# Four squares in flight, a pause before each group of heads, and wider block sums in a hybrid encoder layer

## The chip, the cores and the metric

The kernel runs on one core of one Trainium2 chip. The metric is the time of one execution on the device in microseconds (us). The kernel before takes 2103.46 us, the median of three runs (2101.09 to 2105.57).

## The reference

One encoder layer is applied to two inputs with the same weights: the sample, 1024 tokens, and the prompt, 512 tokens, both of width 2048. Cut to what matters:

```python
def mixer_layer(x, ...):
    h = rms_norm(x, norm_g)
    z = h @ w_in                                  # 2048 -> 5632
    c_val, c_glu, c_gate, q, k, v, a_gate = split(z)
    q, k = apply_rope(q), apply_rope(k)           # 8 heads, 2 key/value heads, head size 128
    conv_out = conformer_conv(c_val, c_glu, ...) * silu(c_gate)   # 31 taps, layer norm, silu, @ w_pw
    attn_out = banded_sink_attention(q, k, v, sink) * silu(a_gate)  # blocks of 128, window 128
    mix = concatenate([conv_out, attn_out]) @ w_out               # 2048 -> 2048
    return x + mix

def encoder(x, ...):
    return rms_norm(mixer_layer(x, ...), final_norm_g)
```

All tensors are float32.

## The kernel before

Every product is made of three matmuls with rounded parts of the operands (high x high, high x low, low x high). The parts are made by `parts`: ScalarE (ACT) copies the high part (L486), VectorE (DVE) subtracts it (L487). The large products of the sample are done by blocks: a `Unit` takes two blocks of 128 output columns, half of the inner dimension and both halves of the tokens, and needs seven products (`STEPS`) instead of eight, of sums of blocks. A product is 4 x 3 = 12 matmuls (L197), a unit 84. After a product `tap` reads PSUM: ACT copies it (L223) or DVE adds it (L243; in `Onto`, the units of the output product, L290). Loads, stores and weights go through SP's queue in the order of the program that a scheduler sets; adding transfers go through POOL.

The order of work is written by hand in `encoder`. First come four stages of units for the sample's input product, `stages[0]` to `stages[3]` (eight units of the convolution's columns, first with one half of the inner dimension and then with the other; then the same for gates, keys, values and queries). Then come the prompt's 44 jobs `pj` (L631), the pointwise products of the convolution in two halves, the output product of the sample in two stages `over[0]` and `over[1]` of eight `Onto` units, and at last the prompt's own end (L1764).

Beside the matmuls run three lanes, `conv`, `attn` and `prep`. A lane holds generators. After every third matmul, `tick(3 * MM)` adds 648 (MM = 216, in ns) times the lane's `rate` to its credit; while the credit is positive, the first generator is stepped and what it yields is taken off. So a `yield 3000` at rate 1.3 is a pause of 3000 / 1.3 ns of this clock. `drain` steps a lane until it is empty, without a pause.

What the change touches:

- `rms_ahead` loads the rows of x by halves of a row block ([128, 1024], 512 KB) into tiles of the pool `F` (seven tiles, shared with everything else that is wide) and squares each on ACT with an accumulated sum (L859; the loads are L852). For the sample it runs on the lane `prep`, behind `sums_ahead`, from the fourth unit of `stages[0]` on at rate 1.3, and the lane is drained ahead of the last unit of that stage. The rate is 1.0 from the next stage on. For the prompt it runs in `stages[2]`.
- `spread_rms` turns the sample's result into a row over all partitions, R (L698 on DVE, L703 on PE, L874 on ACT), in three parts, which are called after the first three steps of the last unit of `stages[0]`. In the same unit `switch` loads and splits the tokens of the next stage, one sum of blocks after each step.
- `group` is the attention of one key/value head and its four query heads: it loads k and v (L1084) and the first block's q (L1096), pauses, splits k and v, and then does the blocks of 128 queries in `attention` (scores L1115, their maximum L1118, exponentials L1129, transposes L1149, products with v L1144). Two groups of the sample run on the lane `attn` from the first prompt job on (rate 1.8), `attention_sums` behind them, and then two groups of the prompt (rate 1.2). The lane is drained ahead of the last unit of `over[0]`.
- `conv_sums` reads the sample's gated convolution from DRAM by pairs of row blocks (L1262), makes the four block sums in place (`sums_in_place`, L1270 to L1273) and stores them for `over[1]`. It runs on the lane `prep` from the second step of the first unit of `over[0]` on, at rate 1.0.

Of the kernel before, what the change touches and what calls it, by code (L numbers as in the profile page):

```python
# [706 lines left out]
class Sequence:  # L707
# [136 lines left out]
    def rms_ahead(self):  # L844
        e, nc = self.e, self.e.nc
        held = deque()

        def load(n):
            if n < 2 * self.B:
                b, h = divmod(n, 2)  # L850
                held.append(e.F([D // 2]))
                nc.sync.dma_start(held[-1], self.xN[b * P : (b + 1) * P, h * D // 2 : (h + 1) * D // 2])  # L852

        load(0)
        load(1)
        yield LOAD
        for n in range(2 * self.B):
            x = held.popleft()
            nc.scalar.activation(x, x, AF.Square, accum_out=self.sq[:, n % 2, n // 2 : n // 2 + 1])  # L859
            load(n + 2)  # L860
            yield 3000
        v = e.small(self.B)
        nc.vector.tensor_tensor(v, self.sq[:, 0], self.sq[:, 1], ALU.add)
        nc.vector.tensor_scalar(v, v, 1.0 / D, RMS_EPS, ALU.mult, ALU.add)
        self.rcol = e.stat[self.s][:, 0 : self.B]
        e.rsqrt(self.rcol, v, self.B)
        yield 15000
# [205 lines left out]
    def group(self, g):  # L1073

        e, nc = self.e, self.e.nc
        if self.s == 0:
            k, v = ([e.T1([self.T]) for _ in range(2)] for _ in range(2))
        else:
            kv = e.F([2, self.T], F32R), e.F([2, self.T], F32R)
            k, v = [(t[:, 0], t[:, 1]) for t in kv]  # L1080
        held = []
        for src in (self.k_d[g], self.v_d[g]):
            held.append(e.A([self.T], F32))
            nc.sync.dma_start(held[-1], src)  # L1084
        self.load_query(g, 0)
        yield e.attn.rate * LEAD
        for dst in (k, v):
            e.parts(dst[0], dst[1], held.pop(0))
            yield 3500
        for b in range(self.B):  # L1090
            yield from self.attention(g, b, k, v)

# [117 lines left out]
class Mix:  # L1210
# [46 lines left out]
    def conv_sums(self):  # L1257
        e, nc = self.e, self.e.nc
        for j in range(HALF):
            x = [e.F([TS]) for _ in range(2)]  # L1260
            for t, k in zip(x, (j, j + HALF)):
                nc.sync.dma_start(t, self.xT[k])  # L1262
            yield 2 * LOAD
            self.sums_in_place(0, j, *x)
            yield 4000

    def sums_in_place(self, g, j, x0, x1):
        e, nc = self.e, self.e.nc
# [517 lines left out]
def encoder(ctx, tc, a):  # L1786
    e = Encoder(ctx, tc, a)
# [10 lines left out]
    stages = [  # L1798
        [plain] + [u(0, False) for u in conv[1:]],
        [u(1, True) for u in conv],  # L1800
        [u(1, False) for u in rest],
        [u(0, True) for u in rest],
    ]
# [83 lines left out]
    stages[0][-1].before.insert(0, e.prep.drain)  # L1887
    rms = sample.spread_rms()
    for step in range(SPREAD):
        stages[0][-1].after.setdefault(step, []).append(lambda: e.urgently(next, rms, None))  # L1890

    pace(stages[1][0], RATES[0])
    pace(stages[2][0], RATES[1])
# [55 lines left out]
    def prepare():  # L1949
        until(lambda: sample.convolved == NC, e.conv)  # L1950
        for half in halves:
            e.prep.add(half.prepare())
        e.prep.add(halves[0].fetch())
        e.attn.add(mix.attention_sums())
        for group in prompt.groups:
            e.attn.add(group)
# [113 lines left out]
```

## Time and profile before

| | |
|---|---|
| median of three runs | 2103.46 us (2101.09 to 2105.57) |
| the profiled execution | 2107.31 us, its span 2105.5 us |
| PE (matmul) busy | 2063.2 us, 98% of the span, 9234 matmuls |
| PE weight loads | 1689.4 us, 80% |
| DVE busy | 1751.4 us, 83% |
| ACT busy | 1043.0 us, 50% |
| POOL busy | 77.1 us, 4% |
| DMA | 494.54 MB, 235 GB/s in the mean |

PE is TensorE's matmuls, PEld its weight loads, SPq the queue of SyncE that issues transfers. A line of the timeline has the start in us, the duration in us, the engine, the source line, the instruction, what it writes and reads (names of tiles without numbers), the count, and in brackets the idle time of the engine just before it and what ended it. A line of groups ends in the busy time in us, the mean duration in ns, and the idle time before. Every source line is that of the kernel before.

### The profile page before, as it was taken

Reading aid. Unit: us, or ns where it says so; the run is one execution under the profiler, and the core shown is the slowest. Engines: PE = TensorE matmul, PEld = TensorE weight load, DVE = VectorE, ACT = ScalarE, POOL = GpSimd, SP = SyncE. Lnnn points to the kernel's source line nnn. Section 1 sums busy time; section 2 is a strip of 40 time slices with the busy share of each in tenths; the row PEclk is TensorE's granted clock in tenths of the full one; section 3 lists DMA queues with packets and bytes.
Section 4 is the critical chain, followed back from the end, with each engine's and each line's share of the span. In section 5 each row is a group of like instructions: output and inputs, shape, how many; then the busy total and the mean of one; then the engine's idle time right before and its main releaser. Section 6 shows DMA issues by size and latency. Waiting matters only on the chain. (4 is left out here: it accounts for less than half of the span.)

```text
span 2105.5 us, 26965 instructions
## 1 busy us (share of the span) xinstructions
PE 2063.2 (98%) x9234; PEld 1689.4 (80%) x9234; DVE 1751.4 (83%) x2855; ACT 1043.0 (50%) x1682; POOL 77.1 (4%) x92
## 2 busy tenths in 40 slices
PE   8999999999999999999999999999999999999996
PEld 6878888888887888788888888878888788788875
DVE  8758798998899999999476777677798988899866
ACT  6476435333454444554455777336554343455444
POOL 0001110000011111100000000000000000000000
PEclk9999999999999999999999999999999999999999
DMA  8988887865577767954455555996789898677898
GB/s 279 313 283 248 205 216 229 295 203 170 180 236 195 169 165 184 276 166 157 151 184 188 179 168 197 319 335 207 237 283 302 273 321 290 207 259 246 293 310 276
DMA packets 269914, 494.54 MB, mean 235 GB/s; under 512 B 23632, under 2 KB 107984, under 8 KB 269776
## 3 DMA queue, kind: packets, MB, share of 16 engines
q1 hardware_dynamic: 257104, 469.75, 67.5%
q0 software_dynamic: 12672, 23.07, 6.8%
q8 instruction: 72, 1.18, 0.2%
q14 instruction: 66, 0.54, 0.1%
HBM read 331.77 MB, written 160.96 MB: 234 GB/s over the span
## 5 line engine op out<-in xcount | busy, mean ns | idle before, releaser
L197 PE MATMUL a<-t,hl 128*128 128x512 f32 x2640 | 634.8, 391 | 8.1 <-ACT u L223 2.6
L197 PEld LDWEIGHTS a<-t,hl 128*128 128x128 f32 x2640 | 494.4, 188 | 116.6 <-ACT u L223 5.5
L486 ACT ACTIVATE hl<-raw 128x1024 fp32r<-128x1024 f32 (+1 forms) x356 | 323.9, 910 | 433.6 <-DVE raw L139 93.9
L487 DVE TENSOR_TENSOR hl<-raw,hl 128x1024 fp32r<-128x1024 f32 (+1 forms) x356 | 369.2, 1038 | 153.5 <-ACT hl L486 152.8
L631 PE MATMUL a<-t,hl 128*128 128x512 f32 x1344 | 328.1, 394 | 0.5 <-DVE hl L487 0.5
L197 PE MATMUL c<-t,hl 128*128 128x512 f32 x1320 | 320.2, 390 | 3.1 <-DVE u L290 2.6
L197 PEld LDWEIGHTS c<-t,hl 128*128 128x128 f32 x1320 | 247.0, 188 | 56.8 <-DVE u L290 4.3
L631 PEld LDWEIGHTS a<-t,hl 128*128 128x128 f32 x1344 | 248.2, 188 | 50.9 <-DVE hl L487 1.0
L999 DVE SCALAR_TENSOR_TENSOR f<-f,c_w_dw,f 128x512 f32<-128x512 f32 x248 | 175.2, 746 | 0.3
L631 PE MATMUL c<-t,hl 128*128 128x512 f32 x672 | 165.5, 394 | 0.0
L962 DVE SCALAR_TENSOR_TENSOR f<-f,c_w_dw,f 128x512 f32<-128x512 f32 x232 | 163.7, 745 | 1.2 <-ACT f L957 1.2
L631 PE MATMUL b<-t,hl 128*128 128x512 f32 x672 | 163.4, 392 | 0.2 <-DVE hl L487 0.2
L197 PE MATMUL b<-t,hl 128*128 128x512 f32 x660 | 160.0, 390 | 0.0
L631 PEld LDWEIGHTS b<-t,hl 128*128 128x128 f32 x672 | 125.0, 188 | 25.3 <-DVE hl L487 0.6
L631 PEld LDWEIGHTS c<-t,hl 128*128 128x128 f32 x672 | 125.1, 189 | 24.4
L197 PEld LDWEIGHTS b<-t,hl 128*128 128x128 f32 x660 | 123.7, 188 | 25.5
L991 DVE SCALAR_TENSOR_TENSOR f<-f,w_both,f 128x512 f32<-128x512 f32 x120 | 89.8, 748 | 1.8
L223 ACT ACTIVATE u<-a 128x512 f32<-128x512 f32 x82 | 48.6, 592 | 57.4 <-PE a L197 55.3
L394 ACT ACTIVATE hl<-raw 128x1024 fp32r<-128x1024 f32 x44 | 46.5, 1056 | 59.6 <-PE a L631 22.3
L223 ACT ACTIVATE g<-a 128x512 f32<-128x512 f32 x78 | 46.2, 593 | 56.1 <-PE a L197 54.1
L1129 ACT ACTIVATE p<-p,tiny 128x384 f32<-128x384 f32 (+1 forms) x96 | 54.6, 570 | 38.3 <-DVE tiny L1126 28.0
L486 ACT ACTIVATE a<-pt 128x512 fp32r<-128x512 f32 x64 | 37.9, 592 | 67.9 <-PE pt L1149 67.6
(332 smaller groups left out, 2561.4 us busy)
## 6 DMA issues: line engine op xcount, KB each, us to landing
raw<-w_in SPq DMA_DIRECT2D x171, 512.0 KB, 5.1
raw<-wsum_P SPq DMA_DIRECT2D x32, 512.0 KB, 4.7
raw<-w_out SPq DMA_DIRECT2D x31, 512.0 KB, 5.5
raw<-w_pw SPq DMA_DIRECT2D x24, 512.0 KB, 4.4
raw<-w_out SPq DMA_DIRECT2D x48, 256.0 KB, 5.3
wsum_P<-raw SPq DMA_DIRECT2D x47, 256.0 KB, 3.4
f<-x_s SPq DMA_DIRECT2D x16, 512.0 KB, 7.3
a<-sum_S SPq DMA_DIRECT2D x24, 256.0 KB, 5.6
```

Source lines behind the costliest of these rows:

```text
L197: nc.tensor.matmul(acc, hl[:, l, o, j, :], toks[j][:, r], start=name in FRESH and j == 0 and q == 0, stop=name in LAST and j == HALF - 1 a ...
L223: nc.scalar.activation(t, bank, AF.Copy)
L394: e.nc.scalar.activation(t[:, 0], raw, AF.Copy)
L486: nc.scalar.activation(hi, x, AF.Copy)
L487: nc.vector.tensor_tensor(lo, x, hi.bitcast(F32), ALU.subtract)
L631: nc.tensor.matmul(job.acc[0], hl[:, l, kk // HALF, kk % HALF, :], r, start=i == 0 and p == 0, stop=i == nk - 1 and p == 2,)
L962: nc.vector.scalar_tensor_tensor(t, h[:, j : j + T], w(j), t, ALU.mult, ALU.add)
L991: nc.vector.scalar_tensor_tensor(m0, odd[:, j : j + H], both(j), m0, ALU.mult, ALU.add)
L999: nc.vector.scalar_tensor_tensor(out, d[:, j : j + H], w(2 * j + k), out if j else m0, ALU.mult, ALU.add)
L1129: nc.scalar.activation(p[:, 0:n], p[:, 0:n], AF.Exp, bias=nm[:, h : h + 1], accum_out=l[:, h : h + 1])
```

## The change

Four edits:

- In `rms_ahead` the sample has four loads of x in flight instead of two; the prompt keeps two.
- In `group` a pause of `e.attn.rate * 4000` is put between the split of k and v and the first block, that is 4000 ns of the lanes' clock at any rate.
- In `conv_sums` the pause after each pair is 20000 instead of 4000.
- In `encoder` the three parts of `spread_rms` follow the second to the fourth step of the last unit of `stages[0]` instead of the first to the third.

```diff
@@ rms_ahead
-        load(0)
-        load(1)
+        ahead = 2 if self.s else 4
+        for n in range(ahead):
+            load(n)
         yield LOAD
         for n in range(2 * self.B):
             x = held.popleft()
             nc.scalar.activation(x, x, AF.Square, accum_out=self.sq[:, n % 2, n // 2 : n // 2 + 1])
-            load(n + 2)
+            load(n + ahead)
             yield 3000
@@ group
         for dst in (k, v):
             e.parts(dst[0], dst[1], held.pop(0))
             yield 3500
+        yield e.attn.rate * 4000
         for b in range(self.B):
             yield from self.attention(g, b, k, v)
@@ conv_sums
             yield 2 * LOAD
             self.sums_in_place(0, j, *x)
-            yield 4000
+            yield 20000
@@ encoder
     rms = sample.spread_rms()
     for step in range(SPREAD):
-        stages[0][-1].after.setdefault(step, []).append(lambda: e.urgently(next, rms, None))
+        stages[0][-1].after.setdefault(step + 1, []).append(lambda: e.urgently(next, rms, None))
```

## The prediction

> **What bounds the kernel now.** I read the head of the page first, then stretches of 20 us, then the matrix engine's waits, and then the timeline round each wait.
>
> ```profile
> span 2105.5 us, 26965 instructions
> PE 2063.2 (98%) x9234; PEld 1689.4 (80%) x9234; DVE 1751.4 (83%) x2855; ACT 1043.0 (50%) x1682; POOL 77.1 (4%) x92
> ...
> 120.00:140.00 20.00, 19.17 (x85) 15.50 (x84) 8.92 (x12) 14.58 (x27) 0.00 (x0) 1.00 0.90 302
> 140.00:160.00 20.00, 17.49 (x69) 13.45 (x68) 15.67 (x43) 15.11 (x27) 0.00 (x0) 0.91 0.72 247
> ...
> 180.00:200.00 20.00, 20.00 (x90) 16.57 (x89) 15.39 (x23) 11.88 (x18) 2.73 (x3) 1.00 0.85 250
> ```
>
> The columns of a stretch are PE, PEld, DVE, ACT and POOL busy, then the granted clock, the DMA share and GB/s. An undisturbed stretch holds 90 matmuls, 0.222 us each, and such stretches fill most of the span. So PE is the bound, and no matmul is taken away by the change. All that can be gained is PE's idle time, 2105.5 - 2063.2 = 42 us, and matmuls slowed by a lower clock. Of the 42 us those at the very start and the very end are not touched. What PE waits for is in the waits of PE; the first column after the colon is the total, the last the longest.
>
> ```profile
> PE c L197 <- DVE u L290: 2.6, 4, 1.2
> PE a L197 <- ACT g L223: 2.5, 1, 2.5
> PE s L1115 <- DVE tiny L1118: 2.5, 1, 2.5
> PE s L1115 <- ACT a L486: 2.2, 1, 2.2
> ```
>
> Three of these four are single waits, so the question is which edit reaches which.
>
> **Four squares ahead.** The first stage ends so:
>
> ```profile
> 124.43 5.76 PE L197 MATMUL a<-t,hl 128*128 128x512 f32 x24 [0.83 <-ACT u L223]
> ...
> 130.71 0.58 SPq L852 DMA_DIRECT2D f<-x_s  x1
> ...
> 136.25 0.33 SPq L120 DMA_DIRECT2D raw<-w_in  x1
> ...
> 136.62 0.91 SPq L852 DMA_DIRECT2D f<-x_s  x2
> ...
> 144.61 1.06 ACT L859 ACTIVATE f<-f 128x1024 f32<-128x1024 f32 x1 [3.65 <-DMA f<-x_s]
> 145.66 0.58 ACT L223 ACTIVATE g<-a 128x512 f32<-128x512 f32 x1
> ...
> 146.29 7.36 PE L197 MATMUL a<-t,hl 128*128 128x512 f32 x24 [2.51 <-ACT g L223]
> ```
>
> The last two loads of x leave at 136.62, after a weight load at 136.25 that stood ahead of them on SP. ACT comes to the fifteenth square, waits 3.65 us for its rows, and the copy of a product out of PSUM (L223) stands behind the square; PE needs that bank and stands 2.51 us. Then 24 matmuls take 7.36 us where the same 24 took 5.76 at 124.43: 1.60 us more, with the clock of the stretch down to 0.91. The wait of 0.83 at 124.43 is of the same kind. Sum: 0.83 + 2.51 + 1.60 = 4.9 us.
>
> [...]
>
> After the change the squares keep their places, but load n+4 is issued where load n+2 was, two squares (6000 of the lane's counter at rate 1.3, 4.6 us) earlier. The last pair then takes the place of the loads before it, of which 130.71 is the last: 5.9 us earlier than 136.62, ahead of the weight load, and 5.9 covers a wait of 3.65. The price is DMA time and SP's queue, past which these loads move:
>
> ```profile
> f<-x_s SPq DMA_DIRECT2D x15, 512.0 KB, 7.4
> raw<-w_in SPq DMA_DIRECT2D x4, 512.0 KB, 6.4
> ...
> 100.00:110.00 10.00, 10.00 (x46) 8.29 (x45) 7.81 (x11) 6.18 (x11) 0.00 (x0) 1.00 0.97 340
> ...
> 130.00:140.00 10.00, 10.00 (x46) 8.26 (x44) 1.69 (x3) 6.76 (x14) 0.00 (x0) 1.00 0.95 321
> 140.00:150.00 10.00, 7.49 (x26) 5.75 (x25) 6.34 (x10) 5.95 (x10) 0.00 (x0) 0.83 0.73 251
> ...
> 120.60 1.23 DVE L487 TENSOR_TENSOR hl<-raw,hl 128x1024 fp32r<-128x1024 f32 x1 [6.24 <-ACT hl L486]
> ```
>
> Two loads are 1.05 MB, at 340 GB/s 3.1 us of DMA time pulled out of 140 to 150, where the share is 0.73, into a stretch of 0.95 and more. Weights behind them land up to 3.1 us later. Cover: the split that ends at 121.83 is first used by the second half of the 24 matmuls, about 127.3, so 5.5 us. So this price is 0 as long as the cover holds, and I take 0, since PE lost no matmul from 100 to 110 at 0.97 (46 in 10 us); its far end is a rival below, and a gain beyond the waits is excluded, since PE cannot run ahead of its own 0.222 us. The prompt keeps its two loads.
>
> **Spreading the rms one step later.** The same instructions move back by one step of 12 matmuls, 2.7 us:
>
> ```profile
> L698 DVE TENSOR_SCALAR u<-c_ident,tinyr 128x128 fp32r<-128x128 f32 x8 | 1.8, 283 | 0.0
> ...
> L703 PE MATMUL s<-u,ones_r 128*128 128x512 f32 x4 | 1.8, 448 | 0.0
> ```
>
> L698 has two such groups, 3.6 us of DVE in all, and these now meet one more set of token splits. They issue no DMA. R is first read in the next stage, five steps on. The stretch in which they fall has DVE at 15.67 of 20, so the cost may be nothing, or less, since the step that they leave has just been waiting for the square root; the other end is the longest wait of PE for DVE's additions above, 1.2 us. I take 0.3 lost, nearer to the room that the stretch shows.
>
> **4000 more before each group of heads.** Both sequences wait at the start of their first group, and not of their second:
>
> ```profile
> 880.00:900.00 20.00, 17.50 (x81) 14.42 (x82) 19.73 (x37) 9.50 (x18) 0.00 (x0) 1.00 0.68 220
> ...
> 891.73 1.03 PE L1115 MATMUL s<-t,a 128*128 128x256 f32 x6 [2.48 <-DVE tiny L1118]
> ...
> 1414.89 1.25 SPq L1096 DMA_DIRECT2D u<-q_d  x2
> ...
> 1420.54 0.63 ACT L486 ACTIVATE a<-u 128x512 fp32r<-128x512 f32 x1 [1.89 <-DMA u<-q_d]
> ...
> 1421.22 0.74 PE L1115 MATMUL s<-f,a 128*128 128x256 f32 x4 [2.22 <-ACT a L486]
> ```
>
> The pause is 4000 ns of the clock that counts 216 ns a matmul, 18.5 matmuls or 4.1 us of PE. A pause issues nothing itself; the k, v and q loads stand ahead of it as before. At 1421 the cause is a transfer, q of 1414.89 landing at 1420.5; 4.1 us of other matmuls ahead cover 2.22 us, and I take all of it. At 891 the cause is DVE with 19.73 of 20 us busy: a full engine is as far behind 4 us later unless what fills it is the split of k and v. From 0 to 2.5; I take a quarter, 0.6.
>
> What the pauses move: two groups of the sample and two of the prompt are in one lane, so the last block comes 4 x 4.1 = 16.5 us later.
>
> ```profile
> 1681.06 0.53 SPq L480 DMA_DIRECT2D att_d<-u  x1
> ...
> 1706.11 5.60 PE L197 MATMUL a<-t,hl 128*128 128x512 f32 x24
> ...
> L1118 DVE CUSTOM_DVE_ANT_0 p<-s,c_mask,c_attn_sink 128x256 f32<-128x256 f32 (+1 forms) x32 | 16.4, 546 | 2.7 <-PE s L1115 2.6
> L487 DVE TENSOR_TENSOR a<-pt,a 128x512 fp32r<-128x512 f32 x20 | 13.7, 687 | 5.6 <-ACT a L486 5.6
> ...
> 1640.00:1660.00 20.00, 19.85 (x97) 16.59 (x98) 20.00 (x40) 5.56 (x9) 0.00 (x0) 1.00 0.81 262
> ```
>
> The last unit of the output's first half begins within the 24 matmuls of 1706.11, at 1708.9, and runs the lane dry; the last block would end at 1697.6, 11 us ahead. But 16.5 us more of attention lies in a stage where DVE is full (20.00). The two groups are of the stretch 1421 to 1682, which holds the prompt's eight blocks (32 reductions, four a block): 30.1 / 8 = 3.8 us of DVE a block, a block every 33 us. So 16.5 us is half a block, 1.9 us of DVE, or a whole one, 3.8, if a block's edge falls so. On a full engine that is 0 to 3.8 us of PE (less than nothing is excluded: no work leaves this stage by the pauses); I take 1.9 lost, the half block.
>
> **Block sums over their stage.** In that stage DVE waits for the sums' rows and holds up the additions that free PSUM:
>
> ```profile
> 1613.87 0.69 DVE L1270 TENSOR_TENSOR f<-f,f 128x512 f32<-128x512 f32 x1 [1.73 <-DMA f<-mix_d]
> ...
> 1632.33 0.32 SPq L1262 DMA_DIRECT2D f<-mix_d  x1
> ...
> 1635.14 0.69 DVE L1270 TENSOR_TENSOR f<-f,f 128x512 f32<-128x512 f32 x1 [2.35 <-DMA f<-mix_d]
> ...
> 1638.42 0.96 PE L197 MATMUL c<-t,hl 128*128 128x512 f32 x3 [1.25 <-DVE u L290]
> ...
> 1640.15 0.74 PE L1144 MATMUL pv<-a,f 128*128 128x512 f32 x2 [0.55 <-DVE a L487]
> ```
>
> Row pairs come one behind the other because the tiles of the pair before are still being stored. With 9000 + 20000 instead of 9000 + 4000 a pair, a pair's buffers are free long before the next is read. The two waits shown take 1.25 + 0.55 of PE, the one at 1613.87 another 0.2: 2.0 us, which I take whole; from 0 to 2.0. The four sums end at 9 + 3 x 29 = 96 us of lane clock, and the seven units to the drain hold about 122, so the drain finds nothing.
>
> **Sum.** -4.9 + 0.3 - 0.6 - 2.2 + 1.9 - 2.0 = -7.5 us. The profiled execution took 2107.31 us (span 2105.5 and 1.8 around it), so it would take 2099.8. That execution lies 3.85 above the median 2103.46; the median becomes 2096.0.
>
> **Rivals.** *The queue was the limit.* If squares wait because DMA is full (0.97 at 100 to 110), loads issued earlier only wait longer, and the 4.9 stay: 2103.46 - 2.6 = 2100.9. For it: the share. Against it: 136.62 came late for SP's order, not for DMA's.
>
> *Weights starve, slower.* The loads of x stand ahead of raw<-w_in, and a weight load that lands past its cover of 5.5 us stops PE. Three units lie in the stretch. A stop of 3.1 us with the 1.60 of slow matmuls is 4.7 us, at three units 14.1, and the 4.9 are not won: 2103.46 - 2.6 + 14.1 = 2115.0. It decides once weights need 6.4 + 5.5 = 12 us to land instead of 6.4. Against it: at 0.97 PE lost nothing from 100 to 110. [...]
>
> *The moved attention eats it.* The pauses move waits but remove none, the sums gain nothing on a full DVE, and the 3.8 us are paid: 2103.46 - 4.9 + 0.3 + 3.8 = 2102.7. For it: 20.00 of 20. Against it: most of that stage's stretches hold their matmuls.
>
> **How the numbers follow.** Forecast 0.60; queue the limit 0.15; attention eats it 0.11; weights starve 0.14. A measurement here tells about 0.2%, 4.2 us, from no change. The forecast lies below 2099.3, faster; I give faster 0.62 (a little of the second case), same 0.24, slower 0.14. Best end: all waits gone at no price, 4.9, 2.5, 2.2 and 2.0, makes 11.6, so 2091.9. The top takes in 2102.7 and the 2.1 us by which a run here lay above the median: 2104.8. The case at 2115 is left out.
>
> **What would show it.** In the changed profile: no wait of a square above 1 us for x_s, PE's wait of 2.51 gone and the clock 1.00 from 140 to 160, with 88 or more matmuls (step one); no L1115 wait near 1430 (step two); L1270 without waits for mix_d and the sums spread to about 1680 (step three); the last att_d store at about 1690 to 1698. Wrong would be: ACT waits for raw<-w_in before 150; a wait for DVE of over 2 us between 1560 and 1710; attention work crowded at the last unit; or single waits of 2 us at new places.

## The result, and the profile after

The changed kernel takes 2112.58 us, the median of 17 runs (2109.03 to 2118.79), against 2106.96 us for the kernel before in 17 runs beside it. The ratio is 1.0025 with a 95% interval of 1.0016 to 1.0034: slower by 5.3 us, where 7.5 us faster was forecast. The profiled execution took 2117.92 us, 5.3 us above its median, so it shows more loss (10.6 us of span) than the medians do.

The head of the page of the changed kernel, and two of its stretches of 20 us (PE, PEld, DVE, ACT and POOL busy, granted clock, DMA share, GB/s):

```profile
span 2116.1 us, 26976 instructions
PE 2067.0 (98%) x9234; PEld 1693.4 (80%) x9234; DVE 1752.1 (83%) x2855; ACT 1044.1 (49%) x1682; POOL 77.2 (4%) x92
...
140.00:160.00 20.00, 17.25 (x74) 13.38 (x73) 15.90 (x43) 16.32 (x29) 0.00 (x0) 1.00 0.76 257
...
1710.00:1730.00 20.00, 17.48 (x72) 14.07 (x71) 15.26 (x24) 12.78 (x21) 0.00 (x0) 0.91 0.91 309
```

The same instructions are there, and PE's idle time has grown from 42 to 49 us. From 140 to 160 it does 74 matmuls, not the 88 that were to show step one. New is the stretch 1710 to 1730 with 72, which in the kernel before held 90, with its transfers already at a share of 0.99:

```profile
1710.00:1730.00 20.00, 20.00 (x90) 16.57 (x89) 18.70 (x29) 16.82 (x28) 0.00 (x0) 1.00 0.99 331
```

The waits of PE in the changed kernel, by what ended them (total, times, longest):

```profile
PE a L197 <- ACT u L223: 3.5, 4, 1.6
PE s L1117 <- ACT a L486: 3.5, 1, 3.5
PE a L197 <- DVE u L290: 3.0, 3, 1.3
PE a L197 <- DVE g L290: 2.5, 1, 2.5
...
PE a L197 <- ACT g L223: 1.7, 2, 1.5
PE s L1117 <- DVE tiny L1120: 1.7, 2, 1.2
```

Line numbers after line 855 have grown by one and after 1089 by two: L1117 is the scores of L1115, L860 the square of L859. The wait for the scores that was to go from 2.22 to nothing is 3.5. The wait of 2.5 for `g` (L290) did not exist before.

The timeline of the changed kernel at the three places, first the squares:

```profile
125.37 5.74 PE L197 MATMUL a<-t,hl 128*128 128x512 f32 x24 [1.63 <-ACT u L223]
...
136.49 0.33 SPq L120 DMA_DIRECT2D raw<-w_in  x1
136.86 0.91 SPq L852 DMA_DIRECT2D f<-x_s  x2
...
144.56 1.06 ACT L860 ACTIVATE f<-f 128x1024 f32<-128x1024 f32 x1 [2.62 <-DMA f<-x_s]
...
146.25 2.11 PE L197 MATMUL a<-t,hl 128*128 128x512 f32 x8 [1.54 <-ACT g L223]
...
1415.64 0.93 SPq L1085 DMA_DIRECT2D a<-k_d  x1
...
1424.89 0.89 PE L1117 MATMUL s<-f,a 128*128 128x256 f32 x4 [3.51 <-ACT a L486]
```

The last pair of x leaves at 136.86, where it left at 136.62, and again behind the same weight load. Nothing has been loaded earlier. The load of k leaves at 1415.64 (before: 1410.97, with the kernel 2 us behind), and the scores still come too early for it.

Then the edge between the two halves of the output product, first the first token loads of the next half in the kernel before, and then the changed kernel:

```profile
1676.36 1.36 SPq L839 DMA_DIRECT2D p<-mix_d  x3
```

```profile
1697.12 0.86 SPq L839 DMA_DIRECT2D p<-mix_d  x2
...
1701.20 0.56 SPq L480 DMA_DIRECT2D att_d<-u  x1
...
1715.67 0.86 SPq L839 DMA_DIRECT2D a<-msum_S  x2
...
1716.57 0.43 SPq L271 DMA_DIRECT2D g<-xT_s  x1
...
1722.91 1.31 ACT L486 ACTIVATE t<-a 128x512 fp32r<-128x512 f32 x2 [2.39 <-DMA a<-msum_S]
...
1724.13 1.04 ACT L486 ACTIVATE hl<-raw 128x1024 fp32r<-128x1024 f32 x1
1725.37 0.69 DVE L290 TENSOR_TENSOR g<-a,g 128x512 f32<-128x512 f32 x1 [3.55 <-issue]
...
1726.20 3.19 PE L197 MATMUL a<-t,hl 128*128 128x512 f32 x7 [2.52 <-DVE g L290]
```

The last attention block is stored at 1701.20 instead of 1681.06. The loads of the next half's tokens (L839), which go into tiles that this block held, leave between 1697 and 1746 instead of 1676 and 1733. In that crowd (DMA share 0.97 from 1716 to 1726) the rows of `g`, issued at 1716.57, are used only at 1725.37, 8.8 us later (the trace has them landed at 1725.29; in the kernel before, rows of `g` issued at 1708.25 took 4.1 us); DVE is idle until then (3.55, for which the row names no releaser), ACT waits 2.39 for token rows with a weight split queued behind them (1724.13), and PE stands 2.52 us and its granted clock is 0.50 for 3.41 us from 1725.69 on.

### The profile page after: what moved, and what is told of

Same layout as the page of the kernel before. It is cut to its first block, busy times and chain, and to the rows that moved or that the text cites. A ratio compares the mean times of both kernels' runs of the same rounds, so it can differ in the third digit from the quotient of the medians.

```text
span 2116.1 us, 26976 instructions
## 1 busy us (share of the span) xinstructions
PE 2067.0 (98%) x9234; PEld 1693.4 (80%) x9234; DVE 1752.1 (83%) x2855; ACT 1044.1 (49%) x1682; POOL 77.2 (4%) x92
## 4 chain that ended last, share of the span: by engine, by line
PE 71%; DMA 10%; DVE 10%; issue 5%; ACT 2%; POOL 1%; SPq 1%; ACTq 0%; DVEq 0%; POOLq 0%
PE a L197 20%; PE a L631 12%; PE c L197 10%; PE c L631 6%; PE b L631 6%; PE b L197 5%; DVE hl L487 2%; PE pv L1146 2%; PE s L1117 2%; PE s L197 2%; PE a L1766 2%; DMA f<-x_s 1%; PE pt L1151 1%; DMA raw<-w_out 1%; DMA raw<-wsum_P 1%
## 5 line engine op out<-in xcount | busy, mean ns | idle before, releaser
L197 PE MATMUL a<-t,hl 128*128 128x512 f32 x2640 | 635.5, 391 | 13.2 <-ACT u L223 3.5
L197 PEld LDWEIGHTS a<-t,hl 128*128 128x128 f32 x2640 | 493.7, 188 | 123.2 <-ACT u L223 6.1
L197 PE MATMUL c<-t,hl 128*128 128x512 f32 x1320 | 321.1, 391 | 1.7 <-DVE u L290 1.3
L197 PEld LDWEIGHTS c<-t,hl 128*128 128x128 f32 x1320 | 248.1, 188 | 54.9 <-DVE u L290 2.5
L197 PE MATMUL b<-t,hl 128*128 128x512 f32 x660 | 160.5, 390 | 0.0
L197 PEld LDWEIGHTS b<-t,hl 128*128 128x128 f32 x660 | 123.7, 188 | 25.4
```

The lines of the kernel that those rows point to most:

```text
L197: nc.tensor.matmul(acc, hl[:, l, o, j, :], toks[j][:, r], start=name in FRESH and j == 0 and q == 0, stop=name in LAST and j == HALF - 1 a ...
```

## The experiments

Eighteen kernels were run, each in five rounds beside the kernel before. The table gives the ratio to before with its interval, and in us how much more (+) time than before the profiled execution took for the same matmuls of a stretch (matmuls weighted by their columns; the stretches are named by their times in before). A single stretch scatters: the fifteen other profiles whose order is that of before up to 165 took 0.5 to 3.3 us less than before for 118 to 165, 1.7 in the mean. So only differences of 3 us and more, or ones that come back in several kernels, are read.

| kernel | ratio (95%) | 118-165 | 1050-1130 | 1400-1450 | 1500-1552 | 1552-1665 | 1665-1765 |
|---|---|---|---|---|---|---|---|
| whole change | 1.0025 (1.0016-1.0034) | -0.5 | 1.1 | 3.0 | 1.9 | -2.9 | 6.5 |
| e1 loads and rms | 0.9996 (0.9984-1.0008) | -0.9 | 0.0 | 2.3 | 0.0 | -2.1 | 0.4 |
| e2 pause | 1.0060 (1.0043-1.0076) | -2.0 | 1.2 | 3.6 | 1.2 | 7.1 | 5.0 |
| e3 sums 20000 | 1.0011 (1.0002-1.0019) | -1.9 | -0.1 | 0.0 | 0.0 | -4.1 | 8.2 |
| e4 pause, prompt | 1.0024 (1.0014-1.0034) | -1.6 | 0.0 | -0.3 | -0.1 | 0.2 | 2.9 |
| e5 pause, sums' stores on POOL | 1.0037 (1.0023-1.0051) | -2.0 | 1.4 | 2.3 | 2.9 | 2.0 | 2.8 |
| e6 sums' stores on POOL | 1.0000 (0.9987-1.0014) | -1.1 | 0.0 | -0.1 | 0.0 | -0.9 | 0.9 |
| e7 pause, sample | 1.0021 (1.0007-1.0035) | -0.5 | 1.2 | 4.8 | -0.1 | -0.8 | 2.2 |
| e8 attention earlier | 1.0033 (1.0021-1.0044) | -2.2 | 0.2 | -1.1 | 2.9 | -1.8 | 0.9 |
| e9 sums 20000 on POOL | 1.0007 (0.9996-1.0018) | -1.1 | 0.0 | 2.5 | 0.0 | -3.7 | 3.0 |
| e10 sums 12000 | 1.0000 (0.9988-1.0011) | -1.8 | 0.0 | 3.2 | 0.0 | -3.8 | 1.5 |
| e11 sums 12000 on POOL | 1.0003 (0.9992-1.0014) | -3.3 | -0.1 | 1.7 | 0.0 | -3.5 | 3.7 |
| e13 x on POOL | 1.0003 (0.9991-1.0015) | -5.3 | 0.0 | 0.6 | 0.0 | 3.2 | 0.3 |
| e14 edge rows on POOL | 1.0010 (0.9999-1.0022) | -2.6 | -0.1 | -0.2 | 0.0 | 0.0 | 3.6 |
| e15 change, edge rows on POOL | 1.0036 (1.0020-1.0052) | -2.4 | 1.4 | 1.7 | 2.3 | -3.2 | 9.3 |
| e16 e13 and e14 | 1.0014 (1.0004-1.0025) | -5.3 | -0.1 | 1.6 | 0.0 | -1.0 | 5.6 |
| e17 last x on POOL | 1.0018 (1.0006-1.0029) | 2.8 | 0.0 | 2.1 | 0.2 | -1.8 | 0.7 |
| e18 e17 and e10 | 1.0014 (1.0003-1.0025) | 1.2 | -0.1 | 0.2 | 0.0 | -2.1 | 4.6 |

(e12 changes the order from 1390 on and is told below.)

### The parts alone

**e1**, four loads ahead and the rms one step later:

```diff
+        ahead = 2 if self.s else 4
...
+            load(n + ahead)
...
-        stages[0][-1].after.setdefault(step, []).append(...)
+        stages[0][-1].after.setdefault(step + 1, []).append(...)
```

> Four loads of x ahead and the rms one step later, without the pause and with the old block sums. The prediction's terms for these two were -4.9 and +0.3, together -4.6 us. The two traces speak against both: every engine has the same instructions in the same order in both kernels up to 876 us. Theory 'nothing moved' (mine): the same program in all but names, so the same time as before, within 2 us, and ACT waits again 2 us or more for the last rows of x. Rival 'the loads are worth their price': -3 to -5 us. Rival 'weights starve': +4 us or more, with ACT waiting for raw<-w_in.

Level with before, as the first theory said. The instructions of every engine come in the same order as before from end to end. Why shows in the trace of before, at the seventh to tenth loads:

```profile
113.91 1.06 ACT L859 ACTIVATE f<-f 128x1024 f32<-128x1024 f32 x1 [0.27 <-DMA f<-x_s]
114.77 2.66 SPq L852 DMA_DIRECT2D f<-x_s  x4
...
117.98 1.06 ACT L859 ACTIVATE f<-f 128x1024 f32<-128x1024 f32 x1 [1.91 <-DMA f<-x_s]
```

The square of 113.91 is the fifth; by 117.4 ten loads have left (two up to 101.38, four from 104.05 to 110.53, and these four). Five are in flight, with a program that asks for two. The scheduler already runs the loads further ahead than that; the text of the program does not set the depth.

**e2**, the pause alone, and **e4** and **e7**, before the prompt's groups and before the sample's alone:

```diff
+        yield e.attn.rate * 4000
...
+        if self.s:
+            yield e.attn.rate * 4000
...
+        if not self.s:
+            yield e.attn.rate * 4000
```

> The pause before each group of heads alone. The prediction's terms were -0.6 -2.2 +1.9 = -0.9 us. Theory 'late attention' (T1): the last block ends about 20 us later (1701 instead of 1681), the tiles that it holds are those into which the rows of the third stage are read, and PE waits for these rows at the stage's edge, 2 us or more near 1726 with a second of half clock; so all of the loss is here, +5 us or more. Rival 'late sums' (T2): the late rows are those of the block sums, so the pause alone costs 0 to 2 us, and the wait near 1726 is gone.

> The pause only before the prompt's two groups; the sample's two groups start as before. The last block then ends about 8 us later than before, not 16.5 to 20. T1: about half of the loss of the full pause, +2 to +4 us, and the wait near 1726 shorter than with the full pause. Rival 'the sample's groups' (T3), by which the loss of the full pause comes from the new waits between 892 and 1425 (1.2, 0.9, 0.7 and 3.5 us with half clock): nothing is lost here, 0 to -2 us, and the wait at 1425 is shorter than the 2.22 us before.

> The pause before the sample's two groups only, the complement of the pause before the prompt's (+0.24%). T3 (the loss is where the sample's groups start): new waits of about 1 us at 892 to 1076, 3.4 us at 1422, +3 us or more by 1450, and little after. T1 (only late attention near the end costs): nothing until 1500, and then the loss of half the shift, +2 to +5 us between 1600 and 1760. If the parts add up, pause (+12.6) less pause before the prompt (+4.1 to +5) leaves +7.5 to +8.5; if less comes out, the two shifts together make a collision that neither makes alone.

The pause alone costs 12.6 us, more than twice the whole change; the prompt's half 5.1, the sample's half 4.4. So each half costs something (both theories were half right), and the 3 us that are left, no more than the intervals allow for, would come only of both together. At the edge e4 and e7 lose 2.9 and 2.2, with the last block stored at 1691.0 and 1692.5; e2, with 1709.1, loses 5.0. The five kernels with neither a later attention nor spread sums nor moved edge loads (e1, e6, e8, e13, e17) lose 0.3 to 0.9 there, so this loss goes with the late attention (T1). The sample's pause also makes a wait of 1.2 to 1.5 us at 1075, in each of the five kernels that have it (T3). The largest loss of e2 was foreseen by neither. The timeline of the pause alone:

```profile
1608.90 4.11 SPq L480 DMA_DIRECT2D msum_S<-f  x4
...
1613.07 0.92 SPq L271 DMA_DIRECT2D u<-xT_s  x2
...
1617.44 0.69 DVE L290 TENSOR_TENSOR u<-a,u 128x512 f32<-128x512 f32 x1 [4.11 <-DMA u<-xT_s]
...
1618.28 4.18 PE L197 MATMUL a<-t,hl 128*128 128x512 f32 x9 [8.74 <-DVE u L290]
```

SP issues four stores of block sums one by one, each when DVE has made its sum, over 4.1 us. The load of `u` stands behind them; DVE waits 4.11 for it and PE 8.74.

**e3**, the wider block sums alone:

```diff
             self.sums_in_place(0, j, *x)
-            yield 4000
+            yield 20000
```

> The wider block sums alone. The prediction's term was -2.0 us. T1: the waits of DVE for mix_d rows go, the attention ends at 1681 as before, and the time is the same or up to 2 us less. T2: the last sums are stored at about 1686 instead of 1656, the rows that are read from them come late, and PE waits 2 us or more between 1710 and 1740: +4 us or more.

Both theories got a part. From 1552 to 1665 it gains 4.1 us and DVE waits for no `mix_d` row there (before: 5.2 us in three waits). Then it loses 8.2 at the edge. The timeline of the wide sums alone:

```profile
1687.41 0.79 SPq L480 DMA_DIRECT2D msum_S<-f  x1
...
1691.11 0.48 SPq L271 DMA_DIRECT2D g<-xT_s  x1
...
1697.08 0.69 DVE L290 TENSOR_TENSOR g<-a,g 128x512 f32<-128x512 f32 x1 [5.25 <-DMA g<-xT_s]
...
1697.92 2.47 PE L197 MATMUL a<-t,hl 128*128 128x512 f32 x6 [2.10 <-DVE g L290]
```

The last sums are now stored between 1682 and 1691, ahead of `g<-xT_s`, which leaves at 1691.11 in a kernel that is 5 us ahead by then. In the kernel before no store of these sums stood in front of it:

```profile
1689.60 0.56 SPq L271 DMA_DIRECT2D g<-xT_s  x1
```

In e3 PE stands 2.10 us at 1698 and 2.50 at 1743. The two parts do not add: pause 0.60% and sums 0.11% would make 0.71%, and the whole is 0.25%. With wide sums in it the pause has no collision at 1618 (the whole change takes 2.9 us less than before from 1552 to 1665, e2 7.1 more), and at the edge the whole loses 6.5, between the 5.0 of the one and the 8.2 of the other.

### Is it the queue of SP?

The same stores issued by POOL, with the pause (**e5**), alone (**e6**), with the wide sums (**e9**); then sums at 12000, on SP (**e10**) and on POOL (**e11**):

```diff
         for name, t in (("S1", d), ("S3", b), ("S2", a), ("S4", c)):
-            e.store(self.sums_d[g, name][j], t)
+            nc.gpsimd.dma_start(self.sums_d[g, name][j], t)
...
-            yield 20000
+            yield 12000
```

> The pause alone, and the sixteen stores of the convolution's block sums issued by POOL instead of SP. In the run with the pause alone PE stood 8.74 us at 1618; ahead of the load that it waited for (u<-xT_s, SP at 1613.07) SP issued four stores of sums from 1608.90 on, each as late as DVE's subtraction for it. Theory 'a store that waits blocks the loads behind it on SP': the load leaves about 4.4 us earlier, the wait falls to 4.4 us or less, and of the pause's +12.6 us 5 or more go. Rival 'DVE or the transfers are late': the wait at 1618 stays at 7 us or more and the time is that of the pause alone.

> The kernel before with nothing but the sixteen stores of the block sums moved from SP to POOL; a control for the run with the pause, and a candidate. Theory of the blocked queue: where the stores hold up no load that is needed soon, as before, little is to be won: 0 to -2 us (the waits of 1.25 and 0.55 near 1640). Rival: a store from POOL costs something itself; then +1 us or more here too.

With the pause, the load no longer waits behind the stores:

```profile
1605.70 0.88 SPq L271 DMA_DIRECT2D u<-xT_s  x1
...
1612.03 0.55 POOL L1276 DMA_DIRECT2D msum_S<-f  x1 [12.69 <-DVE f L1271]
...
1614.16 0.69 DVE L290 TENSOR_TENSOR u<-a,u 128x512 f32<-128x512 f32 x1 [0.56 <-DMA u<-xT_s]
...
1614.99 1.62 PE L197 MATMUL a<-t,hl 128*128 128x512 f32 x3 [4.01 <-DVE u L290]
```

The wait falls from 8.74 to 4.01, below the 4.4 expected, and the stretch from 7.1 to 2.0. The ratio goes from 1.0060 to 1.0037, 4.9 us of the 12.6 (the two intervals still touch). What is left of the wait is the transfer itself: the load leaves at 1605.70, and DVE has its rows only at 1614.16. Alone (e6) the move changes nothing, so the stores cost nothing by themselves; what costs is a load behind them that is needed soon. For this wait that is shown; for the time of the kernel the two intervals leave it likely.

> The wider block sums (20000), their sixteen stores issued by POOL. With the wide sums alone the stretch from 1550 to 1660 gained 4.1 us against before and PE then lost 4.0 at 1698 (behind three stores of the last sums on SP, 1687.4 to 1691.1) and 4.2 at 1743. Blocked queue: the wait of 2.10 at 1698 with its half clock goes, the gain of 1550 to 1660 stays, so 3 to 4 us less than the wide sums alone: -1 to -3 us against before. Rival, late rows: the sums are just as late for those who read them, 1698 and 1743 stay, +2 us as with the wide sums alone.

> The block sums at 12000 a pair instead of 4000 or 20000, on SP as before: the last are then stored some 24 us of the lane's clock before those of the wide version. Theory 'late sums cost, spread sums win': most of the 4.1 us of 1550 to 1660 without the waits at 1698 and 1743, -1 to -4 us. Rival 're-dealing of SP's order': no such rule, a wait of 1 to 3 us somewhere else between 1600 and 1760, -1 to +3 us.

> Both: the block sums at 12000 a pair and their stores on POOL. If the blocked queue is all that the sums cost, this is the best of the kernels, -2 to -4 us. If the transfers or DVE are what is late, no better than either alone.

On POOL the wide sums lose their wait at 1698 (0.0 instead of +4.0 for 1665 to 1710) and keep 3.7 of gain, but the edge still takes 3.0, and the time is level (1.0007). At 12000 it is level on either queue. The five kernels with spread sums and no pause gain 2.1 to 4.1 us from 1552 to 1665, 3.4 in the mean (the six with neither edit, e1, e6, e13, e14, e16 and e17, 0.4 in the mean, from a gain of 2.1 to a loss of 3.2), and all five give 1.5 to 8.2 back by 1765. The theory of the blocked queue explains the wait at 1698 but not the ones at 1726 to 1747, where the token rows themselves are late.

**e12**, the stores of the attention's block sums on POOL, so that k and q can leave earlier:

```diff
     def block_sums(self, g, j, x0, x1):
...
-            e.store(self.sums_d[g, name][j], t)
+            nc.gpsimd.dma_start(self.sums_d[g, name][j], t)
```

> The kernel before, with the stores of the attention's block sums (not the convolution's) issued by POOL. On SP four of them and the two stores of DVE's gate stand between 1405.5 and 1410.9 ahead of the load of k (1410.97), whose late landing, with q's, makes PE's wait of 2.22 us at 1421. Blocked queue: k and q leave 1 to 2 us earlier, the wait falls below 1.2 us, -1 to -2 us in that stretch. Rival: the load waits for its tile or for the DMA engines; the wait stays above 2 us.

A miss, and the most telling one: 1.0047 (1.0031 to 1.0062). k and q do leave earlier, k by 20 us and q by 14:

```profile
1400.36 1.82 SPq L1096 DMA_DIRECT2D u<-q_d  x2
...
1407.61 0.63 ACT L486 ACTIVATE a<-u 128x512 fp32r<-128x512 f32 x1 [0.32 <-DMA u<-q_d]
...
1408.29 1.22 PE L1115 MATMUL s<-f,a 128*128 128x256 f32 x4 [8.84 <-ACT a L486]
```

But the scores have moved forward on PE with them, by 95 matmuls, to where their rows have only just been asked for, and PE stands 8.84 us. Here the place of the scores follows the loads. The pause of 4000 does not move it: in the traces 5771 matmuls other than those of the attention (its scores, transposes and products with v) stand before the first scores of the prompt, in the kernel before and in all kernels with the pause. The pause moves the blocks after that: the last product with v stands after 6720 other matmuls before, 6756 in e4 and in e7, and 6792 in e2 and the whole change. (No longer pause was run.)

**e8**, the opposite sign:

```diff
-        yield e.attn.rate * LEAD
+        yield e.attn.rate * (LEAD - 4000)
```

> The opposite sign: no pause, and 4000 less (5000 instead of 9000) between the loads of a group and its first split, so the lane's last block is about 16.5 us earlier than before instead of later. T1, lateness at the edge costs: the stretch 1700 to 1760 gains or stays, 0 to -3 us; against it the first waits of the groups grow, the one at 1421 from 2.2 to as much as 6.3 us, so in sum +1 to +5. Rival 'any shift re-deals which store stands ahead of which load on SP': a new wait of 2 us or more at a place between 1550 and 1760 where none was, whatever the sign of the shift.

Slower too, 1.0033, 7.0 us. The edge takes 0.9 us, no gain; PE waits 2.63 at 899 (7.0 us are lost from 860 to 920), 2.78 at 1407 and 1.90 at 1561. Neither theory came out as written. The sum is above T1's +5, and between 1550 and 1760, where the rival wanted a new wait of 2 us, there is one of 1.90. What the run shows is that a shift of this lane by 16 us makes new waits the other way too. Lateness at the edge costs, earliness wins nothing there.

### The edge, and the squares

**e14**, **e15** and **e16**: the 28 token loads of the edge issued by POOL, in the kernel before, in the whole change, and with the next edit.

```diff
-            e.nc.sync.dma_start(x, src)
+            getattr(e, "edge", e.nc.sync).dma_start(x, src)
...
+            if seq is mix:
+                e.edge = e.nc.gpsimd
```

> The kernel before, the 28 token loads at the edge of the output's halves (L839 from 1676 on) issued by POOL; PE's order is unchanged. Control for the next: 0 to -2 us, since PE waited for none of them; by the rival that such loads cost more from POOL, +1 us or more.

> The whole change, with the same 28 token loads on POOL. T1, the late attention holds their tiles: they leave no earlier than 1697 to 1745, and the loss at the edge stays (+4 us or more against before between 1710 and 1761), so the time stays at +5 us against before. Rival, SP's order: with a queue of their own, and SP free of them, the wait of 2.52 at 1726 goes, and 4 us or more of the loss with it, so -1 to +2 us against before.

The last transposes of the attention and POOL's first load of the edge, without the change (e14) and with it (e15):

```profile
1674.61 0.60 PE L1149 MATMUL pt<-c_ident,p 128*128 128x128 f32 x4
...
1675.48 0.57 POOL L839 DMA_DIRECT2D p<-mix_d  x1 [807.76 <-PE pt L1149]
```

```profile
1693.36 0.60 PE L1151 MATMUL pt<-c_ident,p 128*128 128x128 f32 x4
...
1694.23 2.57 POOL L839 DMA_DIRECT2D p<-mix_d  x4 [823.84 <-DMA g<-xT_s]
```

POOL has had nothing to do for 800 us, and still the first load leaves 18.7 us later with the change: what holds it is not a queue but its tile `p`, which the last block's transposes read: in both it leaves 0.27 us after they end (1675.21 and 1693.96). (In e15 the row puts the release down to a landing of `g<-xT_s`; in the program the load waits for those transposes, and for no `g<-xT_s`.) The loss at the edge stays (9.3). T1 holds in this. The rival fails: with SP free of these loads PE still waits 2.31 at 1723 and 2.34 at 1747. The control is no gain either (3.6 at the edge, 1.0010). That loads which leave sooner take from the transfers that are needed first would explain it, but is not shown here.

**e13** moves the sixteen loads of x to POOL; PE's order is unchanged:

```diff
-                nc.sync.dma_start(held[-1], self.xN[...])
+                q = nc.sync if self.s else nc.gpsimd
+                q.dma_start(held[-1], self.xN[...])
```

> The kernel before, the sixteen loads of x (f<-x_s) issued by POOL instead of SP; PE's order is unchanged. If SP's order held them (the last pair left at 136.62 behind a store and a weight load, 3 squares ahead of ACT with 7 tiles): the pair leaves 4 us earlier or more, the waits of PE at 124 (0.83) and 146 (2.51, and the half clock after it) go, and the prediction's term of -4.9 us is made here without its edit: -2 to -5 us. If their tiles or the DMA engines held them: they leave and land as late as before, 0. If a load from POOL is dearer, or delays the weights that it passes: 0 to +5 us.

> Both moves to POOL in the kernel before, a candidate: the sum of the two runs alone, since they lie 1500 us apart; -2 to -6 us if the first does what the blocked queue says.

In e13, around the first stage's end (line numbers from 852 on are one higher here and in e17):

```profile
103.49 0.60 ACT L223 ACTIVATE u<-c 128x512 f32<-128x512 f32 x1 [6.14 <-DMA part_conv<-u]
...
104.14 3.01 PE L197 MATMUL c<-t,hl 128*128 128x512 f32 x12 [2.60 <-ACT u L223]
...
128.87 0.53 POOL L853 DMA_DIRECT2D f<-x_s  x1 [2.79 <-ACT f L860]
```

The last load leaves at 128.87 instead of 136.62, as soon as a square has freed its tile, and the waits at 124 and 146 are gone: -5.3 us against before, -3.6 against the mean of the other profiles. But the first loads leave earlier too, the store of `u` (94.64) takes 8.7 us to land instead of 3.1 (94.94 in the kernel before), ACT waits 6.14 for it and PE 2.60 at 104: 2.9 us lost from 95 to 118 here, and 6.1 in e16. In the sum nothing, and e16 is slower (1.0014) with the edge's 5.6.

**e17** moves only the last seven of these loads, **e18** adds the sums at 12000:

```diff
+                q = nc.gpsimd if not self.s and n >= 9 else nc.sync
```

> The kernel before, the first nine loads of x on SP as before and the last seven on POOL; PE's order is unchanged. If the tiles free in time and SP's order was what held the last loads: the last leaves near 129 instead of 136.6, the wait of 2.51 at 146 goes and nothing is lost at 104, -2 to -4 us. If the weights that they pass suffer, ACT waits for raw<-w_in near 145, and the gain is 0 or less.

> The same with the convolution's block sums at 12000 a pair instead of 4000; the candidate. The sum of the two, since they lie 1500 us apart: the run with 12000 alone gained 3.8 us between 1550 and 1660 and lost 1.5 at the edge, but was level as a whole; -2 to -6 us if the first does its part.

Both miss, 1.0018 and 1.0014. The timeline of e17:

```profile
111.73 0.70 POOL L853 DMA_DIRECT2D f<-x_s  x1 [111.28 <-DMA f<-x_s]
...
115.62 1.60 SPq L853 DMA_DIRECT2D f<-x_s  x3
...
127.56 1.06 ACT L860 ACTIVATE f<-f 128x1024 f32<-128x1024 f32 x1 [5.53 <-DMA f<-x_s]
...
129.24 1.22 PE L197 MATMUL a<-t,hl 128*128 128x512 f32 x2 [5.09 <-ACT u L223]
```

The tenth load, on POOL, leaves at 111.73, ahead of the seventh to ninth, which are still behind the weights on SP (115.62) and are needed first. They land late, a square waits 5.53 and PE 5.09. In the kernel before the DMA share from 100 to 130 is already 0.91 (0.97 in the first 10 us). That the load on the second queue took transfer time from those on the first is an estimate from this share and these rows; how the transfers of two queues divide the time is not shown. No kernel of the eighteen is faster than before beyond its interval.

## Why the prediction was wrong

The mechanism failed, and not only the number. Two of the four edits, with -4.9 and +0.3, moved nothing. Of the pause's -2.8 nothing is left in the sum. The block sums made their gain, but they and the pause cost more than that at an edge for which no term stood.

**Four squares, -4.9.** The step that failed is "load n+4 is issued where load n+2 was". The order did not change at all (e1): this line does not set it, and five loads were in flight before; the rows that show it were in the trace. That late loads make these waits was right: with the last loads earlier (e13) the waits and the slow matmuls go (`a` L197 from 98 to 150: 389 ns each, 408 in the kernel before). The term's size was taken from one execution; the fifteen others took 1.7 us less there in the mean, so that 3.2 of 4.9 were to be had. And its price, put at 0 because PE had lost no matmul from 100 to 110, is 2.9 to 6.1 us when the loads really move (by POOL, in e13 and e16): the rival "the queue was the limit" had the share of 0.97 on its side and was given 0.15.

**Spread, +0.3.** Nothing moved. The wait of 1.21 for L698 at 153 that the changed profile has is in e2 as well, which has not this edit.

**Pause, -0.6 and -2.2.** The first is right in kind: 2.48 at 891 becomes 0.95 and 0.51, and is paid back by the new wait of 1.20 at 1076, which the prediction did not look for. The second failed at "4.1 us of other matmuls ahead cover 2.22 us". No matmul came between: the first scores of the prompt keep their place with the pause of 4000, and the five kernels with the sample's pause wait 2.7 to 4.0 there, the thirteen others with the old order up to that place, before among them, 1.65 to 3.9. What the trace had shown was that scores are placed before their rows have landed; this pause did not move them. (The sample's first scores did move, by 18 matmuls, and there the wait at 891 fell.)

**The moved attention, +1.9.** That the blocks come 4 x 18.5 matmuls later was right: 6720 to 6792. The price was sought in the wrong resource. No run shows a part of DVE's 3.8 us a block in it. What the late blocks hold is the tiles `p` and `a`, wanted by the next half's rows from 1676 on: the first load into `p` leaves at 1697.12 instead. That the tile holds this load is shown (e14, e15); that the 2 to 5 us lost at the edge by e2, e4, e5 and e7 come from it is argued from their agreement. The prediction asked only whether the block ended ahead of the last unit, not who waited for its tiles. In e2 the price is SP's queue as well.

**Block sums, -2.0.** The gain is there and larger, 3.4 in the mean of five kernels against 0.4 in those without. The bound "from 0 to 2.0" was the error: it excluded a loss, though the last stores were moved past the loads of `g<-xT_s` at 1689.60 and onto the edge. That queue should have been walked, as the loads of x were.

**Range and chances.** 2104.8 as the top came from a mechanism on DVE that was not the one at work. The result, 1.0025 times 2103.46 or 2108.7, lies above it; slower had 0.14. The two edits that moved anything, the pause and the block sums, both moved work toward one place, the edge from 1676 to 1765, and none of the terms was worked out there. Of the signs named beforehand, "single waits of 2 us at new places" is the one that came: 2.52 at 1726.

What stays open is why the sums at 12000, on POOL, still lose 3.7 at the edge, what makes the 1.2 to 2.9 us from 1500 to 1552 in the whole change, e2, e5, e8 and e15, and how much of the 1.7 to 4.8 us around 1421 is the pause's: kernels with the old order up to that place show -0.3 to 3.2 for that stretch.

## What to carry to other kernels

Before deepening a look-ahead, count what is in flight in the trace (loads issued less consumers begun): if it is more than the program asks for, tiles or a scheduler set the depth, and the edit is empty (five against two here, and e1 is level at 0.9996). When work is moved later, list the tiles that it holds and the stores that it puts ahead of loads on a queue (in e2 four stores went out ahead of the load of `u`, over 4.1 us, and PE stood 8.74), and look up who takes the tile next and which load stands behind the store; in a stage where the DMA share is high, 0.91 from 100 to 130 here, ask what comes late when a transfer leaves earlier: in e13 a store took 8.7 us to land instead of 3.1, in e17 a square waited 5.53 us for its rows. Size a single wait by several executions, since one here was 1.7 us larger than its mean.

## What the runs showed of the hardware

While PE still has matmuls, the granted clock of the kernel before falls once, to 0.50 for 3.41 us from 146.49 on, just after the wait of 2.51 us at 146. That of the changed kernel falls three times, each time to 0.50 for 3.41 us: from 667.55 on, after a wait of 1.79 us at 666; from 1425.31 on, after the 3.51 us at 1425; and from 1725.69 on, within the 2.52 us at 1726. These three starts lie 757.76 and 300.37 us apart, 222.0 and 88.0 times 3.413 us. In e3 the two stretches of 20 us with the waits of 2.10 us at 1698 and 2.50 us at 1743 have a mean clock of 0.91, and the one between them has 1.00. In e2, after the 8.74 us at 1618, nine matmuls took 4.18 us, where nine at 1604.61 took 2.21.

But the waits of 2.48 us at 891 and 2.22 us at 1421 in the kernel before were not followed by a fall: the clock is 1.00 from 891 to 905 and from 1421 to 1430. What decides it is not shown. So a wait of about 2 us carried an extra of 0 or, by the 24 slow matmuls at 146 in the kernel before, some 1.6 us; by the nine of e2 the 8.74 us carried 2.0 us or more.
